# A hybrid trunk on one core: nine instead of eight of the eleven swiglu blocks by seven products, in another order and with other filling

## The chip, the core and the metric

The kernel runs on one core of a Trainium2 chip. The metric is the device time of one execution in microseconds, as the median of several runs. Clock and contention are read from the profile of one execution.

## What is computed

A trunk of two layers works on 256 frames of 2048 numbers, in float32. The first layer mixes tokens by gated linear attention, the second by an indexer with top-k attention; after each mixer comes a swiglu block. The change touches the swiglu alone:

```python
D_MODEL = 2048
SEQ = 256
D_FF = 5632

def swiglu(h, w1, w3, w2):
    return (jax.nn.silu(h @ w1) * (h @ w3)) @ w2

for i in range(2):
    h = rmsnorm(x, norm_mix[i])
    x = x + mixer(h)                  # i = 0: linear attention, i = 1: sparse attention
    x = x + swiglu(rmsnorm(x, norm_ffn[i]), ffn_w1[i], ffn_w3[i], ffn_w2[i])
return rmsnorm(x, norm_final)
```

## The kernel before

**Three matmuls for one.** Every float32 operand is split into a rounded part `h` and the rest `l`, and a product is computed as h·h + h·l + l·h. For a weight tile of 512 rows and 512 columns (1 MB, one tile `raw` of 128 partitions by 2048 numbers) `split_w` (L133) casts `wh` on ScalarE (L137) and subtracts `wl` on VectorE (L138). There are three buffers for each of `wh` and `wl`, and four for `raw`. Weights are loaded by SP's queue, each weight as often as it is used.

**The blocks of the swiglu.** The 5632 columns of w1 and w3 are eleven blocks of 512. For each block the kernel needs two products of the frames (two tiles of 128) with a 2048 by 512 weight. There are two ways to them:

- A *plain* block (`plain_steps`, L458): for w1 and then w3, four weight tiles each; each tile is multiplied with both frame tiles. That is 2 x 4 units of 24 matmuls (2 frame tiles, 4 rows of 128, 3 terms), 192 in all, with 8 weight splits. The results stand in the PSUM tiles `half`. In the eighth unit the block is gated on VectorE (L490 to L492), then turned by TensorE (L501) and split into the tile `g` by ScalarE (L507) and VectorE (L508).
- A *pair* block (`pair`, L373): w1 and w3 are computed at once, by a scheme that needs seven products instead of eight. Its products, in the order A11, F5, F3, A12, F6, N7, N22, are named after the form of the frames that is multiplied. Each is 2 weight tiles with 12 matmuls each (L398), so 168 in all, with 14 splits. Between products the weights are added up: the tiles `va` (w1, upper half) and `vb` (w3, upper half) get big sums on VectorE behind A11 (L411) and F3 (L415), two each, and accumulating transfers on GpSimd's queue into `va` behind F5 and F6 (L419), two each. The loads for the pair (`v`, `g3` and `raw`) are issued at L385. The two sets of homes, v0/v1 and v2/g3, change places from pair to pair, so the next pair's first weight can be loaded when N7 has split its tiles, and the second when N22 has.

**Down.** The product with w2 is done in pieces (`pieces`, L516): for each of four column groups, ScalarE copies x into the two PSUM tiles `down` (L521), each block of the piece adds 24 matmuls (L531 to L533, one weight split), and ScalarE copies the sums back to x (L538). A unit of a piece is one block on one column group, 24 matmuls and one split. The last block's part is done after the stage by `residual`.

**The order.** All of this is written out by hand in `ffn` (L541). `turns` lists the pair blocks; each entry names the block, the slots behind which a filling unit is run, and the items whose units join the waiting list: a number is a plain block, a tuple is a piece with these blocks. Slot 0 is behind A11, slot 6 behind N22, slot 7 is the end of the turn, -1 is ahead of A11. Units are taken from the list in order, so a turn may use units of an item of an earlier turn. A pair block is turned by TensorE (L220) in the turn that follows it, and split into `g0`, `g1` or `g2`, by the block's number modulo 3 (L222 on ScalarE, L223 on VectorE). A split is written in the program where its product or unit is; sums are queued behind the next split on VectorE (`sums_due`). On each engine instructions run in the order written by the scheduler.

Of the kernel before, what the change touches and what calls it, by code (L numbers as in the profile page):

```python
# [55 lines left out]
def trunk(  # L56
# [484 lines left out]
    def ffn(layer, nrm):  # L541
# [48 lines left out]
        def filler(item):  # L590

            if isinstance(item, int):
                return "plain", item, plain_steps((w1, w3), item, nrm.forms, sc, ready)
            return "piece", item, pieces(w2, [made[b] for b in item], ready)

        full = (0, 1, 2, 3, 4, 5, 6, 7)
        turns = ((0, (-1, -1, 0, 1, 2, 4, 5, 6), (1,)), (2, full, ((1, 0),)), (3, full, (4,)), (5, full, ((2, 3),)),
                 (6, full, ((4, 5),)), (7, full, (8,)), (9, full, ((6, 7),)), (10, full, ((8, 9),)))
        for turn, (b, at, items) in enumerate(turns):
            todo.extend(filler(i) for i in items)  # L600
            us = [None] * NT
# [501 lines left out]
    with tc.tile_pool(name="fz0", bufs=1) as fz:  # L1103
        n1.begin(fz)
        residual(gla_w_out[0], down, n1.update)
        down = ffn(0, n1)
        flush()
# [6 lines left out]
    with tc.tile_pool(name="fz1", bufs=1) as fz:  # L1114
        n3.begin(fz)
        residual(dsa_w_out[0], down, n3.update)
        down = ffn(1, n3)
        flush()
# [56 lines left out]
```

## Time and profile before

| | |
|---|---|
| median of 3 runs | 2228.13 us (2227.88 to 2228.15) |
| the profiled execution | 2227.94 us |
| its span, first to last instruction | 2226.2 us |
| mean granted TensorE clock | 0.999 |
| moved by DMA | 493.35 MB, mean 222 GB/s |
| weight splits on VectorE in the swiglus, raw, v and g (L138) | 193, 120 and 40 |
| pair matmuls (L398), plain (L475), pieces (L531 to L533) | 2688, 1152, 1920 |

The profile is of one execution. A group's row shows line, engine, operation, out<-in by the program's names, shape and count; behind the first bar the busy time in us and the mean length of one in ns; behind the second the idle time of the engine just ahead of them and what ended most of it. A row of the waits shows who waited for whom, the sum in us, how often and the longest. A row of the timeline shows start, length, engine, line and, in brackets, the idle time ahead. DMA issue rows show the size of one and the median time from issue to landing.

### The profile page before, as it was taken

What the parts mean: (1) busy time and instruction counts of PE and PEld (TensorE: products, weight loads), DVE (VectorE), ACT (ScalarE), POOL (GpSimd) and SP (SyncE); (2) the same over time, 40 slices, a digit from 0 to 9 for tenths busy, and PEclk for the clock granted to TensorE, in tenths of its full rate; (3) what the DMA queues carried; (4) which work ended last, traced back from release to release, by engine and by line L of the source; (5) the groups of instructions that cost most, each with busy time, mean ns of one, the idle gap of its engine ahead of it and who ended that gap; (6) DMA issues with size and microseconds to landing.
All of it is one profiled execution on the core that took longest, in us unless ns stands there. A gap on an engine that the chain in (4) does not pass through costs nothing.

```text
span 2226.2 us, 25148 instructions
## 1 busy us (share of the span) xinstructions
PE 2207.4 (99%) x10199; PEld 1828.2 (82%) x10199; DVE 1545.1 (69%) x1180; ACT 1289.2 (58%) x1248; POOL 111.3 (5%) x157
## 2 busy tenths in 40 slices
PE   9999999999999999999999999999999999999998
PEld 7888888888888888888888888888888888888886
DVE  6546546887777777877655755557877777787776
ACT  5545445666656665666544445456666666666664
POOL 0000000000000000000100000000000000000000
PEclk9999999999999999999999999999999999999999
DMA  8555465889879879777554554466997897897893
GB/s 293 172 170 178 135 229 179 263 224 314 222 228 307 221 229 315 211 228 231 194 183 142 178 173 159 164 204 196 298 243 238 276 247 228 281 261 214 281 245 114
DMA packets 254773, 493.35 MB, mean 222 GB/s; under 512 B 8201, under 2 KB 20833, under 8 KB 254529
## 3 DMA queue, kind: packets, MB, share of 16 engines
q1 hardware_dynamic: 219856, 423.33, 54.4%
q0 software_dynamic: 33792, 67.11, 17.3%
q8 instruction: 80, 1.31, 0.2%
q10 hardware_dynamic: 1008, 1.31, 0.2%
q14 instruction: 37, 0.30, 0.0%
HBM read 489.59 MB, written 2.12 MB: 221 GB/s over the span
## 4 chain that ended last, share of the span: by engine, by line
PE 95%; DVE 2%; ACT 1%; issue 1%; DMA 0%; SPq 0%; POOL 0%; POOLq 0%; ACTq 0%
PE acc L398 26%; PE half L475 11%; PE acc L206 11%; PE acc L208 11%; PE acc L207 11%; PE down L533 7%; PE down L532 6%; PE down L531 6%; PE tr L220 1%; DVE wl L138 1%; ACT wh L137 1%; PE trq L906 0%; PE po L765 0%; DVE v L411 0%; PE s L750 0%
## 5 line engine op out<-in xcount | busy, mean ns | idle before, releaser
L138 DVE TENSOR_TENSOR wl<-raw,wh 128x2048 fp32r<-128x2048 f32 x193 | 441.4, 2291 | 229.8 <-ACT wh L137 228.9
L197 DVE TENSOR_TENSOR wl<-raw,wh 128x2048 fp32r<-128x2048 f32 (+3 forms) x147 | 317.7, 2164 | 275.7 <-ACT wh L196 275.6
L137 ACT CAST wh<-raw 128x2048 fp32r<-128x2048 f32 x193 | 369.4, 1914 | 203.1 <-PE half L475 71.7
L196 ACT CAST wh<-raw 128x2048 fp32r<-128x2048 f32 (+3 forms) x147 | 265.1, 1807 | 221.1 <-PE acc L208 191.1
L206 PE MATMUL acc<-wh,hh 128*128 128x512 f32 (+3 forms) x832 | 325.4, 391 | 0.0
L208 PE MATMUL acc<-wh,hl 128*128 128x512 f32 (+3 forms) x832 | 317.3, 381 | 0.0
L207 PE MATMUL acc<-wl,hh 128*128 128x512 f32 (+3 forms) x832 | 316.4, 380 | 0.6 <-DVE wl L197 0.6
L138 DVE TENSOR_TENSOR wl<-v,wh 128x2048 fp32r<-128x2048 f32 x120 | 274.0, 2289 | 45.1 <-ACT wh L137 44.8
L137 ACT CAST wh<-v 128x2048 fp32r<-128x2048 f32 x120 | 229.7, 1914 | 71.6 <-PE acc L398 35.3
L532 PE MATMUL down<-wl,g 128*128 128x512 f32 x640 | 249.6, 390 | 1.1 <-DVE wl L138 1.1
L531 PE MATMUL down<-wh,g 128*128 128x512 f32 x640 | 249.6, 391 | 0.9 <-ACT g L507 0.9
L533 PE MATMUL down<-wh,g 128*128 128x512 f32 x640 | 248.5, 390 | 0.6 <-DVE g L508 0.6
L207 PEld LDWEIGHTS acc<-wl,hh 128*128 128x128 f32 x832 | 156.7, 188 | 29.6 <-issue 1.7
L208 PEld LDWEIGHTS acc<-wh,hl 128*128 128x128 f32 x832 | 156.3, 188 | 29.3
L206 PEld LDWEIGHTS acc<-wh,hh 128*128 128x128 f32 x832 | 156.5, 188 | 28.6 <-issue 1.9
L398 PE MATMUL acc<-wh,fhF 128*128 128x512 f32 x384 | 150.8, 393 | 0.0
L398 PE MATMUL acc<-wh,flF 128*128 128x512 f32 x384 | 149.9, 390 | 0.0
L398 PE MATMUL acc<-wl,fhF 128*128 128x512 f32 x384 | 149.6, 390 | 0.0
L532 PEld LDWEIGHTS down<-wl,g 128*128 128x128 f32 x640 | 120.2, 188 | 27.6 <-DVE wl L138 2.8
L531 PEld LDWEIGHTS down<-wh,g 128*128 128x128 f32 x640 | 120.2, 188 | 26.1 <-ACT g L507 1.5
L533 PEld LDWEIGHTS down<-wh,g 128*128 128x128 f32 x640 | 119.9, 188 | 26.2 <-DVE g L508 1.4
L206 PE MATMUL acc<-wh,g 128*128 128x512 f32 x312 | 123.3, 395 | 0.7 <-ACT g L222 0.7
(283 smaller groups left out, 3675.9 us busy)
## 6 DMA issues: line engine op xcount, KB each, us to landing
raw<-in_ffn_w SPq DMA_DIRECT2D x200, 1024.0 KB, 6.2
v<-in_ffn_w SPq DMA_DIRECT2D x48, 1024.0 KB, 8.4
v<-in_ffn_w POOLq DMA_DIRECT2D x48, 1024.0 KB, 9.9
raw<-in_dsa_w_in SPq DMA_DIRECT2D x48, 1024.0 KB, 4.9
raw<-in_gla_w_in SPq DMA_DIRECT2D x40, 1024.0 KB, 5.0
raw<-in_gla_w_out SPq DMA_DIRECT2D x16, 1024.0 KB, 5.0
g<-in_ffn_w SPq DMA_DIRECT2D x16, 1024.0 KB, 8.0
g<-in_ffn_w POOLq DMA_DIRECT2D x16, 1024.0 KB, 13.8
```

The costliest lines, as they stand in the source:

```text
L137: nc.scalar.copy(wh, raw)
L138: v = nc.vector.tensor_sub(wl, raw, wh.bitcast(F32))
L196: a = nc.scalar.copy(wh[:, sl, :n], raw[:, sl, :n])
L197: v = nc.vector.tensor_sub(wl[:, sl, :n], raw[:, sl, :n], wh[:, sl, :n].bitcast(F32))
L206: nc.tensor.matmul(acc[t][:, :n], hi[:, k, ts_], wh[:, k, :n], start=start, stop=False)
L207: nc.tensor.matmul(acc[t][:, :n], hi[:, k, ts_], wl[:, k, :n], start=False, stop=False)
L208: nc.tensor.matmul(acc[t][:, :n], lo[:, k, ts_], wh[:, k, :n], start=False, stop=last)
L398: nc.tensor.matmul(acc, l_[:, k, :], r_[:, j, :], start=start and k == i == 0, stop=stop and k == 7 and i == 2, skip_group_check=not start)
L475: nc.tensor.matmul(acc[bank], l_[:, k, :], r_[:, j, :], start=start and k == i == 0, stop=stop and k == 7 and i == 2, skip_group_check=not ...
L531: nc.tensor.matmul(acc[t], hi[:, k, ts_], wh[:, k, :], start=False, stop=False, skip_group_check=True)
L532: nc.tensor.matmul(acc[t], hi[:, k, ts_], wl[:, k, :], start=False, stop=False, skip_group_check=True)
L533: nc.tensor.matmul(acc[t], lo[:, k, ts_], wh[:, k, :], start=False, stop=last, skip_group_check=True)
```

## The change

`turns` is written anew. Nine blocks are pairs (0, 2, 3, 4, 6, 7, 8, 9, 10) and two are plain (1 and 5); before, eight were pairs and three plain (1, 4 and 8). The pieces are now (0), (1, 2), (3, 4), (5, 6), (7, 8) and (9); before they were (1, 0), (2, 3), (4, 5), (6, 7) and (8, 9). Most turns have six filling units, behind all products but A12; pair 0's turn and pair 2's have five behind products, none behind F5 and A12; pair 10's turn has eight. There are 56 units per layer where there were 64. The list is the same for both layers.

```diff
-        full = (0, 1, 2, 3, 4, 5, 6, 7)
-        turns = ((0, (-1, -1, 0, 1, 2, 4, 5, 6), (1,)), (2, full, ((1, 0),)), (3, full, (4,)), (5, full, ((2, 3),)),
-                 (6, full, ((4, 5),)), (7, full, (8,)), (9, full, ((6, 7),)), (10, full, ((8, 9),)))
+        five, six = (0, 2, 4, 5, 6), (0, 1, 2, 4, 5, 6)
+        turns = ((0, (-1, -1, 0, 2, 4, 5, 6), (1,)), (2, five, ((0,),)), (3, six, ((1, 2),)), (4, six, (5,)),
+                 (6, six, ((3, 4),)), (7, six, ()), (8, six, ((5, 6),)), (9, six, ((7, 8),)),
+                 (10, (0, 1, 2, 3, 4, 5, 6, 7), ((9,),)))
```

VectorE in pair 0's turn of the first layer, before, from F5's two splits on (`v2` and `g3` are va, `v0` and `v1` vb, `raw` with L138 in turn a unit's tile, F3's two, a unit's, A12's two):

```order
L138 TENSOR_TENSOR wl_3115<-v2_3030,wh_3114 128x2048
L138 TENSOR_TENSOR wl_3132<-g3_3032,wh_3131 128x2048
L138 TENSOR_TENSOR wl_3153<-raw_3150,wh_3152 128x2048
L138 TENSOR_TENSOR wl_3188<-raw_3183,wh_3187 128x2048
L138 TENSOR_TENSOR wl_3204<-raw_3185,wh_3203 128x2048
L415 SCALAR_TENSOR_TENSOR v0_3034<-v0_3034,raw_3183 128x2048
L486 TENSOR_TENSOR early_2936<-early_2936,half_2938 128x512
L138 TENSOR_TENSOR wl_3225<-raw_3222,wh_3224 128x2048
L415 SCALAR_TENSOR_TENSOR v1_3036<-v1_3036,raw_3185 128x2048
L138 TENSOR_TENSOR wl_3258<-raw_3253,wh_3257 128x2048
L138 TENSOR_TENSOR wl_3274<-raw_3255,wh_3273 128x2048
```

The same place of the changed kernel:

```order
L138 TENSOR_TENSOR wl_3115<-v2_3030,wh_3114 128x2048
L138 TENSOR_TENSOR wl_3132<-g3_3032,wh_3131 128x2048
L138 TENSOR_TENSOR wl_3155<-raw_3150,wh_3154 128x2048
L138 TENSOR_TENSOR wl_3171<-raw_3152,wh_3170 128x2048
L415 SCALAR_TENSOR_TENSOR v0_3034<-v0_3034,raw_3150 128x2048
L138 TENSOR_TENSOR wl_3190<-raw_3187,wh_3189 128x2048
L415 SCALAR_TENSOR_TENSOR v1_3036<-v1_3036,raw_3152 128x2048
L138 TENSOR_TENSOR wl_3226<-raw_3221,wh_3225 128x2048
L138 TENSOR_TENSOR wl_3242<-raw_3223,wh_3241 128x2048
L486 TENSOR_TENSOR early_2936<-early_2936,half_2938 128x512
```

The unit's split between F5 and F3 is gone, and the plain block's L486 has moved behind A12's splits.

ScalarE at the same place, before, from F3's first cast on (L485 and L487 are the plain block's silu, with the load of a table of functions; L434 copies F5's result):

```order
L137 CAST wh_3187<-raw_3183 128x2048
L434 COPY u_3148<-acc_3113 128x512
L137 CAST wh_3203<-raw_3185 128x2048
L485 ACT_TABLE_LOAD
L485 ACTIVATE early_2936<-half_2937,rstd_3109 128x512
L137 CAST wh_3224<-raw_3222 128x2048
L487 ACTIVATE early_2936<-early_2936,rstd_3109 128x512
L137 CAST wh_3257<-raw_3253 128x2048
L137 CAST wh_3273<-raw_3255 128x2048
L137 CAST wh_3291<-v2_3030 128x2048
L137 CAST wh_3308<-g3_3032 128x2048
```

And in the changed kernel:

```order
L137 CAST wh_3154<-raw_3150 128x2048
L137 CAST wh_3170<-raw_3152 128x2048
L434 COPY u_3148<-acc_3113 128x512
L137 CAST wh_3189<-raw_3187 128x2048
L137 CAST wh_3225<-raw_3221 128x2048
L137 CAST wh_3241<-raw_3223 128x2048
L485 ACT_TABLE_LOAD
L485 ACTIVATE early_2936<-half_2937,rstd_3109 128x512
L137 CAST wh_3259<-v2_3030 128x2048
L487 ACTIVATE early_2936<-early_2936,rstd_3109 128x512
L137 CAST wh_3276<-g3_3032 128x2048
```

The silu and its table have moved from behind F3's casts to between A12's casts and F6's (`v2_3030` and `g3_3032`).

ScalarE at the end of the first layer's swiglu, before (the last two units are two blocks on one column group; `wh` with L196 is the first weight tile of `residual`; L222 is the split of block 10, turned by TensorE behind the last unit):

```order
L538 COPY x02_85<-down0_7108 128x512
L521 COPY down0_7241<-x03_87 128x512
L538 COPY x12_86<-down1_7109 128x512
L137 CAST wh_7247<-raw_7245 128x2048
L521 COPY down1_7242<-x13_88 128x512
L137 CAST wh_7277<-raw_7275 128x2048
L561 ACTIVATE acc_6808<-acc_6808,rq_3111 128x512
L196 CAST wh_7338<-raw_7336 128x2048
```

And in the changed kernel, where these units are two column groups of the piece (9):

```order
L137 CAST wh_7311<-raw_7309 128x2048
L561 ACTIVATE acc_6830<-acc_6830,rq_3111 128x512
L196 CAST wh_7372<-raw_7370 128x2048
...
L538 COPY x02_85<-down0_7269 128x512
L521 COPY down0_7305<-x03_87 128x512
L538 COPY x12_86<-down1_7270 128x512
L222 CAST g1_7341<-tr_7342 128x512
L521 COPY down1_7306<-x13_88 128x512
```

The four copies between two column groups, which stood ahead of the last two units, now stand between them, with one of block 10's splits ahead of the last copy.

## Prediction

> **What bounds the kernel now.** First the page, for the share of each engine and the chain of waits:
>
> ```profile
> span 2226.2 us, 25148 instructions
> PE 2207.4 (99%) x10199; PEld 1828.2 (82%) x10199; DVE 1545.1 (69%) x1180; ACT 1289.2 (58%) x1248; POOL 111.3 (5%) x157
> ...
> PE 95%; DVE 2%; ACT 1%; issue 1%; DMA 0%; SPq 0%; POOL 0%; POOLq 0%; ACTq 0%
> ```
>
> TensorE is busy 99% of the span and is 95% of the chain, so a matmul that goes away should shorten the run by its own pitch, as long as its neighbours are not late. The pitch is read from TensorE's timeline in the block of pair 3, at the first of A11's 24 matmuls and the first of the unit behind them; the transposes of a turned block follow inside that unit:
>
> ```profile
> 561.78 0.39 PE L398 MATMUL acc<-wh,fhA 128*128 128x512 f32 x1
> ...
> 567.22 0.39 PE L475 MATMUL half<-wh,fhA 128*128 128x512 f32 x1
> ...
> 568.59 0.60 PE L220 MATMUL tr<-ident,u 128*128 128x128 f32 x4
> 568.94 0.48 PE L475 MATMUL half<-wh,fhA 128*128 128x512 f32 x1
> ```
>
> 24 matmuls take 567.22 - 561.78 = 5.44 us, 0.2267 us each; the 0.39 us of a row is its length in the pipeline, not its price. A product, and a filling unit, are 24 matmuls each.
>
> Second, TensorE's own waits, because they are what a new order can add or take away:
>
> ```profile
> PE down L532 <- DVE wl L138: 1.1, 4, 0.3
> PE down L531 <- ACT g L507: 0.9, 2, 0.4
> PE acc L206 <- ACT g L222: 0.7, 2, 0.3
> ...
> PE down L533 <- DVE g L508: 0.6, 2, 0.3
> ...
> PE tr L220 <- DVE g L508: 0.3, 1, 0.3
> ```
>
> These eleven belong to the two swiglu stages and their ends: 3.6 us of idle time. The idle time starts only when the 0.39 us of the matmul before is over, so each cost 0.39 - 0.23 = 0.16 us more: 3.6 + 11 x 0.16 = 5.4 us. Third, how much room is below TensorE, from the windows of pair 0's turn (six filling units, none behind A12) and of a later turn with eight:
>
> ```profile
> 406.10:476.80 70.70, 70.70 (x313) 58.55 (x312) 57.91 (x31) 44.30 (x29) 5.38 (x4) 1.00 0.93 279
> ...
> 728.60:811.10 82.50, 82.50 (x369) 68.35 (x368) 62.27 (x33) 53.83 (x46) 5.16 (x4) 1.00 0.85 255
> ```
>
> The columns after the length are busy us of PE, PEld, DVE, ACT and POOL, then clock, DMA share, GB/s. Pair 0's turn already has the spacing that the change gives to the others, and TensorE is busy through all of it at clock 1.00; but VectorE is at 82% and the DMA engines at 93%.
>
> **The change part by part.** *The matmuls.* A pair block has 7 x 24 = 168, a plain block 8 x 24 = 192; per swiglu one plain block becomes a pair, so 24 go per layer and 48 in all: 48 x 0.2267 = 10.9 us, all on the path. The 56 units that are left (of 64) are the same work. The Trainium skill, TensorE: Matmul & The Clock Gate, section Back-to-back issue gap, gives about 131 ns as the sustained spacing at N=512; by it 48 matmuls would be 6.3 us. The trace's 0.2267 us decides here, and the sum goes by it.
>
> *What VectorE and ScalarE get.* A pair has 14 weight splits and four big sums, a plain block 8 splits:
>
> ```profile
> L138 DVE TENSOR_TENSOR wl<-raw,wh 128x2048 fp32r<-128x2048 f32 x193 | 441.4, 2291 | 229.8 <-ACT wh L137 228.9
> L137 ACT CAST wh<-raw 128x2048 fp32r<-128x2048 f32 x193 | 369.4, 1914 | 203.1 <-PE half L475 71.7
> ...
> L521 ACT COPY down<-x 128x512 f32<-128x512 f32 x80 | 47.3, 591 | 15.5 <-DVE early L490 12.1 <-DVE early L491 2.4
> L538 ACT COPY x<-down 128x512 f32<-128x512 f32 x80 | 46.7, 584 | 108.0 <-PE down L533 107.1
> L411 DVE TENSOR_TENSOR v<-v,v 128x2048 f32<-128x2048 f32 x16 | 36.5, 2284 | 0.0
> ...
> L222 ACT CAST g<-tr 128x512 fp32r<-128x512 f32 x40 | 22.7, 586 | 15.3 <-PE tr L220 15.0
> ```
>
> Per layer that is 10 x 2.29 = 23 us more for VectorE and 6 x 1.91 = 11.5 us for ScalarE, and 16 copies of 0.59 us, since two pieces now have one part. With six units a turn VectorE has 20 splits and four sums, 24 x 2.29 = 55 us, beside 312 x 0.2267 = 70.7 us of matmuls: it fits, as in pair 0's turn. So these cost nothing on average, and the question is single places, where a split can't be ready two weight tiles ahead. There are three.
>
> *A: pair 0's turn, where the unit behind F5 goes.* VectorE and ScalarE there now:
>
> ```profile
> 425.07 2.29 DVE L138 TENSOR_TENSOR wl<-raw,wh 128x2048 fp32r<-128x2048 f32 x1 [0.91 <-ACT wh L137]
> 427.28 2.28 DVE L415 SCALAR_TENSOR_TENSOR v<-v,raw 128x2048 f32<-128x2048 f32 x1
> 429.49 0.68 DVE L486 TENSOR_TENSOR early<-early,half 128x512 f32<-128x512 f32 x1
> 430.08 2.28 DVE L138 TENSOR_TENSOR wl<-raw,wh 128x2048 fp32r<-128x2048 f32 x1
> ...
> 441.68 1.92 ACT L137 CAST wh<-g 128x2048 fp32r<-128x2048 f32 x1 [0.80 <-PE acc L398]
> ...
> 443.63 2.29 DVE L138 TENSOR_TENSOR wl<-g,wh 128x2048 fp32r<-128x2048 f32 x1 [0.43 <-ACT wh L137]
> ```
>
> With three buffers a cast starts when TensorE is done three weight tiles earlier, and its subtraction 443.63 - 441.68 = 1.95 us behind it. Today F3's second split follows a long unit and starts early. Let F3's matmuls start at 0: without the unit, its second half's cast waits for F5's first half to end, at -2.7; subtraction from -0.6 to 1.6 (VectorE's pitch is 427.28 - 425.07 = 2.2), sum to 3.8, the next unit's subtraction to 6.0. TensorE wants it with that unit's second matmul, at 5.44 + 0.23 = 5.7. That and the handover make 0.4 to 0.5 us late. Behind A12 the plain block's first silu now falls where A12 and F6 follow each other without a unit, and with it a table load; the cast of A12's second half also waited for its load:
>
> ```profile
> 425.41 1.28 ACT L485 ACT_TABLE_LOAD   x1 [0.36 <-PE half L475]
> 426.70 0.69 ACT L485 ACTIVATE early<-half,rstd 128x512 f32<-128x512 f32 x1
> ...
> 436.00 1.91 ACT L137 CAST wh<-raw 128x2048 fp32r<-128x2048 f32 x1 [0.64 <-DMA raw<-in_ffn_w]
> ...
> raw<-in_ffn_w SPq DMA_DIRECT2D x200, 1024.0 KB, 6.2
> ...
> g<-in_ffn_w POOLq DMA_DIRECT2D x16, 1024.0 KB, 13.8
> ```
>
> From that load on (itself 6.2 us, beside an accumulating transfer of up to 13.8), cast, table load, silu and F6's cast are 1.9 + 1.3 + 0.7 + 1.9 = 5.8 us in a row on ScalarE, and F6's subtraction comes 0 to 1.1 us late, as the load lands 5 us after its issue or behind the accumulation. I take 0.9, since the row shows the load already waited for. What F6's other half and the next unit's cast queue behind this adds up to 0.6 at most. A is 0.5 + 0.9 = 1.4 us, between 0 and 2.2.
>
> *B: pair 2's turn.* Two products without a unit between them meet two L223 and three early pieces (0.6 us pitch, row 429.49) on VectorE. Counted from A11's start, the first unit's subtraction ends at 1.95 + 2.2 + 0.1 = 4.3 us (its cast waits for the unit before A11); then VectorE has 7 big passes and 5 small ones up to the unit behind F3, 7 x 2.2 + 5 x 0.6 = 18.4 us, and is done at 22.7. TensorE wants it after A11, unit, F5 and F3 with four groups of four transposes (568.94 - 568.59 = 0.35 us each): 4 x 5.44 + 1.4 + 0.2 = 23.4. It is not late by itself, but ScalarE's two copies into the unit's sums stand ahead of a cast. I take 0.3 us, between 0 and 2.0 (the two waits of this turn now, with some more).
>
> *F: the stage's end.* Piece (9) has one part, so its units behind N22 are two column groups in a row, on the same two sums. Behind the last but one, L538 must empty each sum and L521 fill it before its matmuls: L538, L521, L538, L222, L521, 0.58 + 0.59 + 0.58 + 0.59 + 0.59 = 2.9 us from some 0.4 before that unit's end (its first sum is done three matmuls early). The second sum is ready 2.5 us after the end; TensorE, with six transposes (0.5) and three matmuls (0.7), would be at it after 1.2. I take 1.3 us, between 0.5 and 1.9. The block is turned earlier, so L206's wait at the end should go; it is in the 5.4 us.
>
> *Costed at nothing, at most 0.5 us a layer together.* From plain block to piece in pair 6's turn N7, which has no sums, covers the early passes. Block 6 takes the buffer g0 while piece (3, 4) still reads block 3 in it, so its two L222 wait on ScalarE behind N22's casts for that piece; behind them wait only the next unit's cast and what follows it, and that cast waits for the same unit anyway: 0.1 + 2 x 0.59 + 1.95 + 2.2 = 5.4 us after it, against 5.44 + 0.23.
>
> *The moved transfers.* Each load and each accumulation moves with its product, SP's queue and POOL's keep their order but for the plain block's eight loads a layer:
>
> ```profile
> v<-in_ffn_w SPq DMA_DIRECT2D x48, 1024.0 KB, 8.4
> v<-in_ffn_w POOLq DMA_DIRECT2D x48, 1024.0 KB, 9.9
> ```
>
> The next pair's second weight is loaded when N22 has split the old one, and added behind A11: N22, unit, A11 are 3 x 5.44 = 16 us for 8.4. F5's accumulations have four products and units until F6, 22 us, at worst for 13.8; from F6 to N22 nothing changes. SP waits for v in front of raw loads that are four buffers ahead. So none of it is on the path, unless transfers stretch: the last rival.
>
> *What goes.* The old places of the eleven waits (plain to piece at F5) are gone with the old order: -5.4 us, at least 0.
>
> Sum: 2227.94 (the profiled execution: span 2226.2 and 1.74 around it) - 10.9 - 5.4 + 2 x (1.4 + 0.3 + 1.3) = 2217.6; the median of the runs is 0.2 above that execution, so 2217.8. With all added terms at their tops, 2 x 6.6 = 13.2, it is 2224.8; with none, 2211.6.
>
> **The rivals.** *Nothing new is late* (the bottoms of A, B and F): 2211.6 plus 0.2, 2211.8. For it: pair 0's turn shows no wait now. Against: A is worked out from just that turn with one unit fewer.
>
> *Small lateness at every column group.* The unit behind a finished column group is split just in time:
>
> ```profile
> 526.79 2.29 DVE L138 TENSOR_TENSOR wl<-raw,wh 128x2048 fp32r<-128x2048 f32 x1 [3.51 <-ACT wh L137]
> ...
> 529.37 0.39 PE L532 MATMUL down<-wl,g 128*128 128x512 f32 x1
> ```
>
> It ends at 529.08, 0.29 us ahead. There are 24 such units per layer afterwards (20 before). If ScalarE's queue, with fewer units to catch up in, costs each 0.5 us, 0.2 of it shows: 48 x 0.2 = 9.6 us, 2227.4: no change. Against: the cast there waits for TensorE, not for the queue's backlog.
>
> *Slower: transfers take the lead.* Turn by turn a pair needs eight loads and four accumulating transfers in about 70.7 us instead of 82.5. Pair 0's window is 93% of its length, 65.8 us of transfer time; a later turn has one load fewer. If in a row of such turns that grew past 70.7 us, each would wait, at F6 and N22 for the accumulated halves and at A11 for the next pair's. At 1.5 us in each of 16 turns it gives 2217.8 + 24 = 2241.8; it decides from about 72 us of transfers a turn. For it: the window's 93%. Against: that window ran without a wait on TensorE. The Trainium skill, DMA: Bandwidth & Descriptors, section Bandwidth, puts the limit of one core's HBM at about 358 GB/s; 279 GB/s in that window is below it, so by the page there is room, while the engines' share of 93% says there is little.
>
> *The change does not do what it says*: the order could have kept the stages' length by moving matmuls. It has 48 fewer on TensorE, so I give it 0.01, at no change.
>
> **How the numbers follow.** A measurement of this kernel can tell about 0.2%, 4.5 us, from no change. My forecast has 0.66, nothing new late 0.12: both faster, 0.78. Small lateness 0.16 and the change without effect 0.01: the same, 0.17. Transfers: 0.05, slower. The range has to hold the forecast with its bounds, nearly to 2211.6 below and to 2224.8 above; from 2213 to 2225 it leaves out the transfers, the small lateness and part of the case with nothing late.
>
> **What would show it.** Right: in the groups 3024 matmuls of L398 for 2688 and 768 of L475 for 1152; each swiglu stage shorter by about 5 us; TensorE waits on a wl at the unit behind F3 in pair 0's turn, and on L521 at the stage's end; DMA share near 0.9 in the turns without a wait on v or g. Wrong: TensorE waits in most turns on wl, a chain with more than 2% of DVE or ACT, or wh casts that wait for v or g transfers.

## The result, and the profile after

| | before | after |
|---|---|---|
| median of the runs (4 each) | 2228.01 us (2227.86 to 2228.15) | 2215.59 us (2215.48 to 2216.34) |
| the profiled execution, its span | 2227.94, 2226.2 us | 2215.48, 2213.7 us |
| ratio of the runs, 95% interval | | 0.9945 (0.9933 to 0.9957) |

The change takes 12.4 us off: 2.2 us more than forecast, inside the range, and faster by more than 0.2%. The page of the changed kernel, first the span, the engines and the chain:

```profile
span 2213.7 us, 25142 instructions
PE 2195.1 (99%) x10151; PEld 1819.4 (82%) x10151; DVE 1589.8 (72%) x1200; ACT 1326.8 (60%) x1294; POOL 121.6 (5%) x165
...
PE 96%; DVE 1%; ACT 1%; issue 1%; DMA 1%; SPq 0%; POOL 0%; POOLq 0%; ACTq 0%
```

TensorE has 10151 matmuls and transposes for 10199, 48 fewer, and stays 99% busy. VectorE went from 69% to 72%. Next the windows of the two swiglu stages, from the first unit's matmul to the first L206 behind them. Columns as in the prediction: length, busy us of PE, PEld, DVE, ACT and POOL, clock, DMA share, GB/s. Before:

```profile
394.30:1062.14 667.84, 665.95 (x2977) 549.35 (x2975) 515.05 (x285) 424.29 (x344) 43.51 (x38) 1.00 0.84 251
1527.64:2195.27 667.63, 666.00 (x2978) 549.40 (x2976) 514.84 (x285) 424.26 (x344) 42.67 (x34) 1.00 0.84 250
```

And after; the third row is the turn of pair 4, the fourth 9 us of pair 0's turn, to which we come back:

```profile
394.15:1055.63 661.48, 660.01 (x2953) 545.23 (x2952) 538.02 (x295) 442.31 (x365) 48.68 (x42) 1.00 0.88 259
1521.13:2182.75 661.62, 660.04 (x2954) 545.27 (x2952) 538.01 (x295) 442.52 (x366) 47.84 (x38) 1.00 0.88 259
620.00:691.60 71.60, 71.60 (x324) 59.32 (x322) 59.08 (x33) 45.29 (x33) 5.16 (x4) 1.00 0.91 268
424.00:433.00 9.00, 9.00 (x41) 7.43 (x40) 8.82 (x5) 2.89 (x3) 0.00 (x0) 1.00 1.08 292
```

The stages are 6.4 and 6.0 us shorter: all of the gain is there. In a later turn TensorE is busy for 71.60 of 71.60 us, with the DMA engines at 91%. What TensorE waits for in the stages:

```profile
PE acc L398 <- DVE wl L138: 1.6, 2, 0.8
PE acc L398 <- ACT u L434: 1.4, 2, 0.7
```

The eleven waits of before are gone. Four new ones stand in their place, two in each layer, both in pair 0's turn. TensorE's timeline around them, F3's first matmul and F6's second:

```profile
422.06 0.39 PE L398 MATMUL acc<-wh,flF 128*128 128x512 f32 x1
423.13 0.50 PE L398 MATMUL acc<-wh,fhF 128*128 128x512 f32 x1 [0.68 <-ACT u L434]
423.46 0.39 PE L398 MATMUL acc<-wl,fhF 128*128 128x512 f32 x1
...
439.85 0.39 PE L398 MATMUL acc<-wh,fhF 128*128 128x512 f32 x1
441.01 0.50 PE L398 MATMUL acc<-wl,fhF 128*128 128x512 f32 x1 [0.77 <-DVE wl L138]
```

From start to start F3's matmul comes 1.07 us behind the one before, 0.84 more than the pitch; F6's 1.16, 0.93 more. In the second layer they are 0.84 and 0.95, and A12's second half is 0.26 late: 3.8 us in all. So the sum is -10.9 - 5.4 + 3.8 = -12.5 us, which is the difference of the spans. That it closes to the tenth is in part chance: terms of 0.1 to 0.2 us are left out of it, such as 0.1 us at the matmul behind each wait, of the old ones and of the new.

F3's wait is for a PSUM bank. F3 goes on in the bank b2 that holds F5's result, and L434 must first copy that result out. Before, a unit stood between F5 and F3 and gave it the time. F6's wait has ScalarE ahead of it; its timeline from F3's end on:

```profile
422.49 0.59 ACT L434 COPY u<-acc 128x512 f32<-128x512 f32 x1 [0.80 <-PE acc L398]
...
432.92 1.91 ACT L137 CAST wh<-raw 128x2048 fp32r<-128x2048 f32 x1 [4.81 <-DVE wl L138]
434.85 1.28 ACT L485 ACT_TABLE_LOAD   x1
436.15 0.69 ACT L485 ACTIVATE early<-half,rstd 128x512 f32<-128x512 f32 x1
436.74 1.89 ACT L137 CAST wh<-v 128x2048 fp32r<-128x2048 f32 x1
```

The cast of A12's second tile starts after 4.81 us of idle time. Two things end at 432.8 us, just ahead of it: VectorE's subtraction of A12's first tile, which the row names, and the load of the second tile; e9 will tell them apart. Behind the cast stand the table load, the plain block's silu and F6's first cast, without a gap, as the prediction had them. The first theory after the result was therefore: **the bank** (L434) makes F3 late, and **the table load** makes F6 late. The rival: not the table, but **A12's second weight tile** is late, and the table only adds to it. The Trainium skill, ScalarE: Activation LUTs, section What ACT_TABLE_LOAD costs, gives 1283 ns for the load, as here, and some 1380 ns of drain besides; no row here shows a drain, since the silu starts 0.02 us behind the load.

### The profile page after: what moved, and what is told of

The parts are those of the page before. It is cut to its first block, busy times and chain, and to the rows that moved or that the text cites. A ratio compares the mean times of both kernels' runs of the same rounds, so it can differ in the third digit from the quotient of the medians.

```text
span 2213.7 us, 25142 instructions
## 1 busy us (share of the span) xinstructions
PE 2195.1 (99%) x10151; PEld 1819.4 (82%) x10151; DVE 1589.8 (72%) x1200; ACT 1326.8 (60%) x1294; POOL 121.6 (5%) x165
## 4 chain that ended last, share of the span: by engine, by line
PE 96%; DVE 1%; ACT 1%; issue 1%; DMA 1%; SPq 0%; POOL 0%; POOLq 0%; ACTq 0%
PE acc L398 30%; PE acc L206 11%; PE acc L208 11%; PE acc L207 11%; PE half L475 7%; PE down L531 7%; PE down L532 7%; PE down L533 7%; PE tr L220 1%; PE trq L907 0%; PE po L766 0%; DVE wl L138 0%; PE s L751 0%; ACT wh L137 0%; PE po L1080 0%
## 5 line engine op out<-in xcount | busy, mean ns | idle before, releaser
L138 DVE TENSOR_TENSOR wl<-raw,wh 128x2048 fp32r<-128x2048 f32 x185 | 422.7, 2291 | 196.4 <-ACT wh L137 196.1
L137 ACT CAST wh<-raw 128x2048 fp32r<-128x2048 f32 x185 | 353.9, 1913 | 172.8 <-PE half L475 54.2
L196 ACT CAST wh<-raw 128x2048 fp32r<-128x2048 f32 (+3 forms) x147 | 265.3, 1807 | 214.4 <-PE acc L208 190.2
L138 DVE TENSOR_TENSOR wl<-v,wh 128x2048 fp32r<-128x2048 f32 x132 | 301.3, 2288 | 36.5 <-ACT wh L137 35.4
L206 PE MATMUL acc<-wh,hh 128*128 128x512 f32 (+3 forms) x832 | 325.4, 391 | 0.0
L137 ACT CAST wh<-v 128x2048 fp32r<-128x2048 f32 x132 | 252.5, 1915 | 72.5 <-PE acc L398 27.8
L531 PE MATMUL down<-wh,g 128*128 128x512 f32 x640 | 250.2, 391 | 0.0
L206 PEld LDWEIGHTS acc<-wh,hh 128*128 128x128 f32 x832 | 156.5, 188 | 28.5 <-issue 1.9
L398 PE MATMUL acc<-wh,fhF 128*128 128x512 f32 x432 | 169.9, 393 | 1.4 <-ACT u L434 1.4
L398 PE MATMUL acc<-wl,fhF 128*128 128x512 f32 x432 | 168.5, 390 | 1.6 <-DVE wl L138 1.6
L398 PE MATMUL acc<-wh,flF 128*128 128x512 f32 x432 | 168.3, 390 | 0.0
L531 PEld LDWEIGHTS down<-wh,g 128*128 128x128 f32 x640 | 120.1, 188 | 24.9 <-ACT down L521 0.4
L419 POOL DMA_DIRECT2D v<-in_ffn_w x52 | 67.3, 1294 | 1118.0 <-DVE wl L138 1118.0
## 6 DMA issues: line engine op xcount, KB each, us to landing
g<-in_ffn_w SPq DMA_DIRECT2D x18, 1024.0 KB, 10.9
```

The source lines that it names most:

```text
L137: nc.scalar.copy(wh, raw)
L138: v = nc.vector.tensor_sub(wl, raw, wh.bitcast(F32))
L196: a = nc.scalar.copy(wh[:, sl, :n], raw[:, sl, :n])
L206: nc.tensor.matmul(acc[t][:, :n], hi[:, k, ts_], wh[:, k, :n], start=start, stop=False)
L398: nc.tensor.matmul(acc, l_[:, k, :], r_[:, j, :], start=start and k == i == 0, stop=stop and k == 7 and i == 2, skip_group_check=not start)
L531: nc.tensor.matmul(acc[t], hi[:, k, ts_], wh[:, k, :], start=False, stop=False, skip_group_check=True)
```

## Experiments

Each kernel is the changed one with the edit shown (its main lines), except where it says otherwise; their line numbers can be a few higher. The medians of the kernel before were 2228.05, 2228.01, 2227.99 and 2228.03 us beside the four groups of runs, so the times can be set beside 2215.59.

| | median (lowest to highest), us | new TensorE waits in the stages |
|---|---|---|
| changed kernel | 2215.59 (2215.48 to 2216.34) | L434, F6 |
| e1 table early | 2213.82 (2213.35 to 2215.03) | L434, A12 in one layer |
| e2 F3 in its own bank | 2214.11 (2213.77 to 2214.82) | A12, 1.0 and 1.8 us |
| e3 e1 and e2 | 2214.81 (2213.02 to 2215.62) | A12, 0.7 us twice (fastest run) |
| e4 before, unit from F5 to A12 | 2232.42 (2232.14 to 2233.92) | L434, the unit behind A12 |
| e5 F3's sum early | 2216.31 (2215.95 to 2217.61) | L434, A12, F6, smaller ones |
| e6 e5 and e2 | 2216.04 (2215.59 to 2216.62) | A12, F6 |
| e7 one unit ahead of A11 | 2221.58 (2220.19 to 2223.12) | A11, the unit behind it, F6 |
| e8 ten pairs | 2317.81 (2315.41 to 2322.94) | 4.1 to 4.9 us at N22 in twelve turns, L434, smaller ones |
| e9 A12's second tile in g2 | 2212.72 (2212.54 to 2213.35) | L434, and one of 0.2 us |
| e10 e9 and e2 | 2211.04 (2210.82 to 2211.09) | none |
| e11 e9 and e6 | 2210.59 (2210.42 to 2211.73) | none |
| e12 e8, L450 earlier | 2264.03 (2262.08 to 2268.29) | many, none above 1.9 us |

**e1: the table loaded early.**

```diff
         todo = deque()
         made = {}
+        nc.scalar.activation(warm, x[1][2][:, 0:8], AF.Silu)
```

> The changed kernel with one small silu of 8 columns more per layer, in the mixer's tail, so that the table of functions is loaded about 60 us ahead of the plain block's first silu. Theory (the table load between A12's second cast and F6's first cast makes F6's split late): without the 1.28 us load F6's first subtraction ends about 0.9 us earlier, at the time when TensorE wants it, so both waits at F6 go and nothing else moves: 2 x 0.9 = 1.8 us less than the changed kernel, about 2213.8 us. Rival (the load of A12's second weight tile is what is late, and the table load only fills that time): F6's wait stays, 2215.6 us. Either way the wait of F3 for L434's copy stays at 0.68 us in each layer.

Measured 2213.82 us, on the theory's number: F6's waits are gone, L434's stay. But now one wait of 0.3 us is at A12's second half. So the table is one link of the chain, and its head is still open.

**e2: F3 in a bank of its own, in pair 0's turn.**

```diff
-        product(b2, vc, "F3", False, True, minus(vb, vc))
+        f3 = bank() if own else b2
+        product(f3, vc, "F3", own, True, minus(vb, vc))
...
-        nc.vector.tensor_add(w, w, b2)
+        nc.vector.tensor_add(w, w, f3)
+        if own:
+            nc.vector.tensor_add(w, w, y)
```

> The changed kernel, but in pair 0's turn F3's product has a PSUM bank of its own, and VectorE adds one term more to w. Theory (F3's first matmul waits for L434 to copy F5's result out of the same bank, and that wait pays for the late splits behind it): the two waits of 0.68 us for L434 are gone, but of their 0.84 us each only a part shows, since then the splits are late: 0.3 to 0.5 us at the unit behind F3, the lateness that the prediction had there, and at A12's second half, whose load lands at the same time as before whatever TensorE does. The silu stands ahead of A12's second cast in this kernel, so the wait at F6 moves there. In all 0.4 to 0.7 us less per layer, 2214.2 to 2214.8 us. Rival (the copy is a wait like any other and nothing is queued behind it): the full 2 x 0.84 = 1.7 us less, 2213.9 us, with F6's waits as they were and no new wait on a wl.

Measured 2214.11 us, 0.1 below the expected range. No wait for L434 is left, so the bank was its cause; but two waits of 1.0 and 1.8 us have come up at A12's second half, where the silu now stands ahead of the cast. Of what the bank gives, 2 x 0.84 us and 0.1 for each matmul behind, a part is eaten behind it, as the theory said.

**e3: both.** 

> Both edits together: F3 in its own PSUM bank in pair 0's turn, and the table of functions loaded in the mixer's tail. Theory (after both, only splits and A12's second load are in the way): no wait for L434, none at F6 but perhaps 0.1 us, and about 0.4 us late at the unit behind F3 or at A12's second half: 1.1 to 1.3 us less per layer than the changed kernel, 2213.0 to 2213.4 us, the fastest of the four. Rival (the two waits are independent and both go fully): 2 x (0.84 + 0.93) = 3.5 us less, 2212.1 us. If it is no faster than the table load alone, then what sets this turn is A12's second load.

Measured 2214.81 us as the median, but from 2213.02 to 2215.62: a wider spread than any kernel with so little waiting has here, and we didn't find its reason. The profiled execution is the one of 2213.02 us and has two waits of 0.7 us, both at A12's second half. With the table and the bank out of the way A12 is still late, which points to A12's second load, as the expectation's last sentence has it; with this spread the medians alone don't settle it. Independent waits that go fully are not what the trace shows.

**e4: the kernel before with the unit moved.**

```diff
-        turns = ((0, (-1, -1, 0, 1, 2, 4, 5, 6), (1,)), (2, full, ((1, 0),)), (3, full, (4,)), (5, full, ((2, 3),)),
+        turns = ((0, (-1, -1, 0, 2, 3, 4, 5, 6), (1,)), (2, full, ((1, 0),)), (3, full, (4,)), (5, full, ((2, 3),)),
```

> The kernel before, with one edit: in pair 0's turn the unit that stood behind F5 stands behind A12. So F5 and F3 follow each other as in the changed kernel, but A12 and F6 do not. Theory (without a unit between them F3 waits for L434's copy out of F5's bank): TensorE waits 0.68 us for L434 once in each layer, 0.84 us by the start of the matmul, none at F6 and none on a wl behind F3: 1.7 us slower than before, 2229.7 us. Rival (the prediction's: F3's second split and the unit's behind it are late): a wait on a wl of 0.3 to 0.5 us behind F3, none for L434, 0.9 us slower, 2228.9 us.

Measured 2232.42 us, slower than both said. TensorE's waits in pair 0's turn of the first layer:

```profile
PE half L475 <- DVE wl L138: 0.8, 1, 0.8
PE acc L398 <- ACT u L434: 0.7, 1, 0.7
```

L434's wait is there as the theory had it, and none at the unit behind F3. But there is also one of 0.8 us at the unit that now stands between A12 and F6. So F6 is not late because a unit is missing ahead of it, as the prediction argued: whatever comes behind A12 is late. What went missing is the unit ahead of F3, which also gave A12's loads 5.44 us. The four waits of both layers come to 3.1 us from start to start; the rest of the 4.4 us is not explained.

**e5 and e6: A12's second load issued earlier**, e6 with the bank as well. The load goes into the raw buffer that F3's first tile leaves, when F3's first sum has read it:

```diff
-        product(b2, vc, "F3", False, True, minus(vb, vc))
+        product(b2, vc, "F3", False, True, minus(vb, vc, first))
```

`minus` then writes the first of the two sums at once, not behind the next split.

> The changed kernel with one edit: in pair 0's turn the first of F3's two big sums on VectorE (L415, which reads F3's first weight tile) stands ahead of F3's first subtraction, where VectorE was idle for 1.7 us, and not behind its second one. The tile is then free 4.5 us earlier, and the load of A12's second weight tile into it is issued at about 421.8 us of the span, not at 426.3. Theory (A12's second load is what makes this place late, and the table load between A12's casts and F6's only adds to it): that load lands before its cast could start, the waits at A12's second half and at F6 are gone though the table is loaded where it was, and with the 0.2 to 0.4 us at A12 and 1.05 us at F6 that is 1.3 us per layer, 2.7 in all: 2212.9 us. Rival (the table load alone makes F6 late): F6's waits stay at 0.77 us, 2215.6 us. The wait of F3 for L434 stays in both.

> The same edit, and F3 in a PSUM bank of its own in pair 0's turn. Theory: no TensorE wait is left in the two swiglu stages, neither for L434 nor for a wl, since with the sum out of the way the unit's subtraction behind F3 is no longer late either: 0.95 us per layer less than with the sum alone, 2211.0 us, the fastest of all and near the case of the prediction in which nothing new is late (2211.8). Rival (the lateness moves on to another place, as it did when only the bank was changed): a wait on a wl of 0.5 to 1 us at the unit behind F3 or at A12, 2212 to 2213 us.

Both were no faster than the changed kernel, 2216.31 and 2216.04 us: the theory of the buffer fell. The load's issue (start, length, engine, line) and its time to landing, first in the changed kernel, with the second of F5's two accumulating transfers, the one into g, behind it:

```profile
426.27 0.37 SPq L385 DMA_DIRECT2D raw<-in_ffn_w  x1
...
raw<-in_ffn_w SPq DMA_DIRECT2D x1, 1024.0 KB, 6.5
...
g<-in_ffn_w POOLq DMA_DIRECT2D x1, 1024.0 KB, 12.6
```

Then with the sum early:

```profile
421.99 0.37 SPq L385 DMA_DIRECT2D raw<-in_ffn_w  x1
...
raw<-in_ffn_w SPq DMA_DIRECT2D x1, 1024.0 KB, 11.5
...
g<-in_ffn_w POOLq DMA_DIRECT2D x1, 1024.0 KB, 14.7
...
424.00:433.00 9.00, 9.00 (x41) 7.42 (x40) 6.92 (x4) 3.02 (x2) 0.00 (x0) 1.00 1.09 284
```

Issued 4.3 us earlier, it landed at 421.99 + 11.5 = 433.5 us of the span, for 426.27 + 6.5 = 432.8. The DMA engines are full from 424 to 433 us in both kernels (shares of 1.08 and 1.09), mostly with F5's accumulating transfers; a plain load issued into that takes its share away from the one into g (14.7 us for 12.6) and is itself no sooner. So the theory for the next kernels: it is **the order of the transfers**. A12's second load must be issued ahead of the accumulations, not only ahead of its place.

**e7: one unit ahead of A11 only, and the unit back behind F5.**

```diff
-        turns = ((0, (-1, -1, 0, 2, 4, 5, 6), (1,)), ...
+        turns = ((0, (-1, 0, 1, 2, 4, 5, 6), (1,)), ...
```

> The changed kernel with pair 0's unit back behind F5, and only one unit ahead of A11. Theory (a unit between F5 and F3 covers L434's copy and the late splits, and what was won ahead of A11 is lost there): no wait for L434, and none or little at F6, 2 us less per layer; but A11's second weight tile, whose load is issued late in the mixer's tail, is late by about 1.9 us per layer, a wait of TensorE on the wl of a g tile at A11: 2215.6 us, no change. Rival (that load would be there in time): 2211.5 us.

Measured 2221.58 us, slower by 6.0. The wait at A11 is there (1.2 us), but behind it, within the unit, one of 2.1 us for a cast, and F6's wait of 0.7 us is still there. That the stage's start has no room is shown; but its price was put at about half (1.9 us a layer, where TensorE lost 1.4 us from start to start at A11 and 2.2 behind it), and that a unit behind F5 would clear F6 was wrong.

**e8: ten pairs**, with four units in most turns.

```diff
+        four = (0, 2, 4, 6)
+        turns = ((0, (-1, -1, 0, 2, 4, 5, 6), (1,)), (2, (0, 2, 4, 5, 6), ((0,),)), (3, four, ((1, 2),)), (4, four, ()),
+                 (5, four, ((3, 4),)), (6, four, ()), (7, four, ((5, 6),)), (8, four, ()),
+                 (9, (0, 2, 4, 5, 6), ((7, 8),)), (10, (0, 1, 2, 4, 5, 6, 7), ((9,),)))
```

> Ten blocks by seven products, only block 1 plain, with four filling units in most turns (behind A11, F3, F6 and N22), five or seven in the others: 48 matmuls fewer again, 10.9 us, and about 62 us of matmuls per turn. Theory (below TensorE there is no room for this): the transfers of a turn, some 60 us of the DMA engines' time by the changed kernel's windows, and the splits no longer fit; the halves that are accumulated behind F6 come 14 us after their issue and are split about 1.6 us late at N22, so TensorE waits on a wl at N22 and A11 in seven turns per layer, 22 us or more in all: slower than the changed kernel by 5 to 20 us, 2220 to 2235 us. Rival (only single places count, as the prediction had it, and transfers are hidden): 2215.6 - 10.9 + some 5 us for waits like those of pair 0's turn, 2205 to 2210 us.

Measured 2317.81 us, slower by 102: the direction was expected, the size by far not. TensorE's waits, and a window over five of its turns:

```profile
PE down L531 <- ACT wh L137: 52.0, 12, 4.9
PE acc L398 <- ACT u L434: 10.8, 16, 0.7
PE acc L398 <- DVE wl L138: 8.1, 18, 0.8
...
620.00:980.00 360.00, 331.43 (x1409) 265.65 (x1408) 276.88 (x147) 216.44 (x171) 28.37 (x22) 0.97 0.84 239
```

One wait repeats in twelve turns, for 52 of the 72 us. The DMA engines are at 84%, less than in the changed kernel: on the average there is room. The place is N22; TensorE's and VectorE's rows there in one turn, and the accumulating transfer of the half of `va` that N22 needs last:

```profile
731.76 0.60 PE L220 MATMUL tr<-ident,u 128*128 128x128 f32 x4
736.84 0.73 PE L531 MATMUL down<-wh,g 128*128 128x512 f32 x2 [4.48 <-ACT wh L137]
737.96 0.79 PE L398 MATMUL acc<-wh,fhN 128*128 128x512 f32 x1 [0.39 <-DVE u L450]
...
735.02 2.29 DVE L138 TENSOR_TENSOR wl<-g,wh 128x2048 fp32r<-128x2048 f32 x1 [4.27 <-ACT wh L137]
737.23 0.68 DVE L450 TENSOR_TENSOR u<-u,acc 128x512 f32<-128x512 f32 x1
...
g<-in_ffn_w POOLq DMA_DIRECT2D x1, 1024.0 KB, 14.9
```

N22's first matmul waits for L450, which takes N7's result out of the bank that N22 goes on with. L450 stands on VectorE behind the subtraction of N22's second half, and that half lands 14.9 us after its transfer was issued behind F6. Between F6 and N22 now stand N7 and one unit, where the changed kernel has N7 and two, and that is too short. Two matmuls of the next unit (L531) were put ahead of N22 and wait too, for a cast that stands behind that half's cast on ScalarE; most of the idle time is counted there. So two ways lead from the late half to TensorE, and they end about 1 us apart.

The wait has an aftermath. TensorE's granted clock (the column behind POOL's) in the 4.2 us behind it:

```profile
736.80:741.00 4.20, 3.77 (x9) 2.73 (x10) 3.31 (x3) 0.00 (x0) 0.00 (x0) 0.59 1.05 406
```

From 741 to 745 us it is 1.00 again. Behind the waits that end at 666, 806 and 874 us it is 0.50, 0.61 and 0.50 in the same 4.2 us.

**e9, e10, e11: A12's second tile in g2.** This buffer is free until block 2 is turned, so its load can be issued before F5's accumulating transfers. e10 adds the own bank, e11 the early sum too.

```diff
-        vd = load(wa, 1, stream)
+        vd = load(wa, 1, (stream[0], (res, "g2", 1) if first else stream[1]))
```

> The changed kernel with one edit: in pair 0's turn A12's second weight tile is loaded into g2, which is free until block 2 is turned, and not into the raw buffer that F3's first tile leaves. Its load then needn't wait for that buffer and is issued ahead of F5's two accumulating transfers, where the DMA engines stand idle around 410 us of the span. Theory (formed from the kernel whose sum was early: there the load was issued 4.3 us earlier and landed no earlier, since the DMA engines were busy with the accumulating transfers until 432 us; so it is the order of the transfers that makes A12's second load, and behind it the silu with its table and F6's split, late): the tile is there by 420 us, the waits at A12's second half (0.2 to 0.4 us) and at F6 (1.05 us) go though the table stays where it is, 1.3 us per layer, 2212.9 us. Rival 1 (the table load alone makes F6 late): F6's waits stay, 2215.6 us. Rival 2 (transfer time is only handed on): the accumulations end some 2.5 us later, and TensorE waits for a wl of the accumulated g tile at F6, 2215 to 2217 us. The wait for L434 stays in all.

> The same home for A12's second tile, and a PSUM bank of its own for F3 in pair 0's turn. Theory: with that load early, what the bank alone could not give is given: no wait for L434, none at A12 and F6; the unit behind F3 is split up to 0.45 us late, which other matmuls moved ahead of it cover, as they did in the kernel with the bank and the early table: 2.2 us per layer less than the changed kernel, 2211.2 us. Rival (the lateness moves on again): a wait on a wl of 0.5 us or more at the unit behind F3 or at F6, 2212 to 2214 us.

> All three edits of pair 0's turn: A12's second tile in g2, F3 in its own PSUM bank, and F3's first sum ahead of F3's subtractions. Theory: no lateness is left even behind F3, 2211.0 us, the fastest with the one before, and within 1 us of it. Rival (the early sum costs something by itself, as in the two kernels with it that were no faster): 1 us or more slower than the kernel before this one, with a wait on a wl at F3 or at the unit behind it.

Measured 2212.72, 2211.04 and 2210.59 us, each within 0.5 us of the theory's number. ScalarE in e9 at the same place, from the cast of A12's second tile on:

```profile
428.99 1.92 ACT L137 CAST wh<-g 128x2048 fp32r<-128x2048 f32 x1 [0.80 <-PE acc L398]
431.76 1.28 ACT L485 ACT_TABLE_LOAD   x1 [0.84 <-PE half L475]
433.05 0.69 ACT L485 ACTIVATE early<-half,rstd 128x512 f32<-128x512 f32 x1
434.43 1.92 ACT L137 CAST wh<-v 128x2048 fp32r<-128x2048 f32 x1 [0.69 <-PE half L475]
```

The cast now waits for TensorE alone and starts 3.9 us earlier. It also starts ahead of VectorE's subtraction of A12's first tile (430.62 us here), so that was not what held it before: the load was. Table and silu stand where they stood in the order, and F6's cast waits for TensorE too. That the table alone makes F6 late is refuted: it takes both, the late load and the table behind it, and F6's wait goes when either is moved (e1, e9). Refuted is rival 2 as well: the accumulating transfers were issued 0.7 us later and landed at most 0.8 us later. e10 is 1.7 us faster than e9, twice the 0.84 us of L434's wait: with the load early, the bank gives its full price. e10 and e11 have no wait above 0.1 us in either stage and are the fastest: e11 against the kernel before 0.9923 (0.9911 to 0.9936), 5.0 us below the changed kernel. Between e10 and e11 the runs tell no difference.

**e12: ten pairs, with L450 ahead of that subtraction.**

```diff
-            for c in range(2):
-                wh, wl = split_w(raws[c])
+            for c in range(2):
+                with behind((first.ins,) if first is not None and c else ()):
+                    wh, wl = split_w(raws[c])
...
+        add = nc.vector.tensor_add(y, y, b3)
+        product(b3, va, "N22", False, True, None, add)
```

> The kernel with ten pairs, with one edit: in every pair L450, which takes N7's result out of the PSUM bank that N22 goes on with, stands ahead of the subtraction of N22's second half on VectorE, where it stood behind it. Theory (of the 102 us that ten pairs cost, most came from this: N22's first matmul waits for L450, L450 stands behind a subtraction, and that waits for the accumulating transfer of the g tile, which lands 14.9 us after its issue): N22 starts when N7 and the transposes are done, and waits only in its middle, for a wl, about 2.0 us; of some 5.2 us lost at N22 in each of twelve turns 3.1 go, 37 us in all, and the clock recovers a little: 2270 to 2282 us, still far slower than the changed kernel. Rival (the late half holds N22 in any case): no more than 10 us less, 2308 us or more.

Measured 2264.03 us: 54 us less, where 37 were expected, and below the expected range. The rival is wrong. In TensorE's order the unit's two matmuls no longer stand ahead of N22, so the edit took away both ways at once and doesn't tell them apart. What is left at N22 is the late half itself, 0.9 to 1.8 us a turn, and 0.4 us for L450. TensorE's waits, and the window of one of its turns:

```profile
PE acc L399 <- DVE wl L138: 25.8, 34, 1.8
PE acc L399 <- ACT u L435: 10.8, 16, 0.7
...
700.00:770.00 70.00, 66.85 (x294) 53.83 (x293) 55.42 (x29) 42.86 (x34) 5.16 (x4) 1.00 0.89 265
```

The clock is 1.00 where e8 had 0.97, over the whole run 0.998 for 0.987. The waits in the stages fell from 72 to 43 us, 29 us, less than expected; the clock's 1.1% of 2314 us is some 25 us, an estimate from the two means; together they are the 54. So the theory undervalued the clock; the clock was not changed by itself. The Trainium skill, TensorE: Matmul & The Clock Gate, section Why this matters for your kernels, warns of a slower clock from idle gaps of more than about 3 us. The two kernels agree with it: in the stages gaps of 4.1 to 4.9 us in e8, with the clock near half behind them, and none above 1.9 in e12.

## Why the prediction was right, point by point

- **The matmuls, -10.9 us: right.** 48 went, at the same pitch, and the whole difference closes with them. By the 131 ns of the Trainium skill, TensorE: Matmul & The Clock Gate, section Back-to-back issue gap, which the prediction set against the trace, 4.6 us of the gain would have no source.
- **The eleven old waits, -5.4 us: right**, all gone.
- **A, pair 0's turn, forecast 1.4 us a layer: measured 1.8 and 2.1**, below the top of 2.2. The step that failed is its first half, the 0.5 us of a late split at the unit behind F3. The lateness was computed rightly, but it isn't on the path. It can be seen where the bank is out of the way, in e10: TensorE's rows at the start of that unit

```profile
427.55 0.39 PE L478 MATMUL half<-wh,fhA 128*128 128x512 f32 x1
427.78 0.39 PE L478 MATMUL half<-wh,fhN 128*128 128x512 f32 x1
428.01 0.39 PE L398 MATMUL acc<-wh,fhA 128*128 128x512 f32 x1
428.29 0.50 PE L478 MATMUL half<-wl,fhA 128*128 128x512 f32 x1
```

  The unit's first matmul with wl stands 0.74 us behind its first, not 0.23: two matmuls that need no wl, one of A12's among them, were put in between, and the wait that is left is 0.05 us. In the changed kernel the wait for L434 covers the lateness as well. The step that the prediction lacked is that wait: F3 and F5 share a PSUM bank, and between them L434 needs about 1 us, which a unit used to give it. That cost 0.84 us a layer; e2 shows the cause. So it is luck that the first half came out near: a wait that the prediction didn't have stands in for one that isn't there.
- **A's second half, 0.9 us at F6: 0.93 and 0.95 measured**, at the place and through the chain that was named, load, cast, table, silu, cast. Its reason was half right. "Since the row shows the load already waited for" was the point: e9 removes the waits with the load alone and leaves the table. "Where A12 and F6 follow each other without a unit" was not: e4 has a unit there and waits all the same.
- **B, pair 2's turn, 0.3 us: nothing.** No wait is there. "It is not late by itself" was right, and the 0.3 us added to it were not needed.
- **F, the stage's end, 1.3 us: about 0.2**, below its own lower bound of 0.5. This is the term that was mis-sized most, 2.2 us over two layers. The copies run as worked out; ScalarE behind the last but one unit, and TensorE, from the transposes on:

```profile
1048.65 0.59 ACT L538 COPY x<-down 128x512 f32<-128x512 f32 x1 [2.27 <-PE down L533]
1049.27 0.59 ACT L521 COPY down<-x 128x512 f32<-128x512 f32 x1
...
1050.75 0.60 ACT L521 COPY down<-x 128x512 f32<-128x512 f32 x1
...
1049.13 0.82 PE L220 MATMUL tr<-ident,u 128*128 128x128 f32 x6
1049.91 0.50 PE L531 MATMUL down<-wh,g 128*128 128x512 f32 x1
...
1051.41 0.61 PE L531 MATMUL down<-wh,g 128*128 128x512 f32 x2
```

  From the first copy to the end of the last they take 2.7 us, to 1051.35. But TensorE doesn't come to the second sum after six transposes and three matmuls: seven matmuls of the first sum are put ahead, and it comes at 1051.6, just behind the copy. What is left is at the first sum: its first matmul stands at 1049.91, just behind the copy that fills it (to 1049.86), some 0.2 us later than six transposes would let it. The prediction took the order in which the program is written for the order on the engine.
- **What was costed at nothing** cost nothing: no other wait in the stages.
- **The rivals.** *Nothing new late* (2211.8) isn't what happened, but e10 and e11 show that it can be had, at 2211.0 and 2210.6. (By the bottoms that it names, F's 0.5 us would belong in it, 2212.8; its number leaves F out.) *Small lateness at every column group*: no wait on a `down` tile is left. *Transfers take the lead*: not turn by turn; the third window row shows TensorE without a gap at a DMA share of 0.91. Yet its mechanism decides at one place, A12's second load, for 9 us in which the engines are full. e8 shows that its turning point was put in the wrong measure: not 72 us of transfers a turn, but whether one accumulating transfer lands in the time between the products on both sides of it. The prediction cited a limit of about 358 GB/s from the Trainium skill, DMA: Bandwidth & Descriptors, section Bandwidth, by which there was room. This row of the changed kernel, from 433 us on, moves 402 GB/s, so that limit doesn't hold here. The same section gives about 358 GB/s as the share when both cores of an HBM domain stream, and its table, taken with one core alone, reaches 425 GB/s for large transfers; this kernel runs on one core, and the table is nearer:

```profile
433.00:441.00 8.00, 7.24 (x31) 5.37 (x29) 5.18 (x3) 7.97 (x7) 0.00 (x0) 1.00 1.05 402
```

So the forecast was 2.2 us too high: F and B were put 2.8 us too high in the two layers and A 1.0 too low, which makes 1.8; the other 0.4 us are not resolved. That the errors had opposite signs is luck.

## What to carry to other kernels

When work that stood between two products is moved, ask not only whether their operands are ready, but also who must still read the PSUM bank that the second goes on with, and whose transfers get less time. Count transfers place by place: here a load that shared the engines with accumulating transfers landed only behind them, though it was issued 4.3 us earlier; a buffer that let it go ahead of them helped. And read lateness from the order on the engine, where independent matmuls may have been put into the gap, not from the order in the program.

## What the runs showed of the hardware

- A wait of TensorE costs more than its idle time: 0.68 us idle at F3 made 0.84 us from start to start, and the next matmul then came 0.33 us behind, not 0.23 (423.13 to 423.46).
- From issue to landing an accumulating transfer of 1 MB took 9 us as the first of two and 12.6 to 14.9 as the second, issued some 2 us later, where plain loads ahead of them took 5.1 (e9, median of four); a plain load of 1 MB issued into them took 11.5 (e5). With accumulating transfers alone under way the DMA engines were full at 209 GB/s (424 to 428 us of the changed kernel), with plain loads alone at 402 (433 to 441).
- Waits of 4.1 to 4.9 us once a turn went with a granted clock of 0.987 over the run (e8), waits below 1.9 us with 0.998 (e12). In e8 the clock is 0.50 to 0.61 in the 4.2 us behind such a wait, and back at 1.00 in the next 4 us behind two of the four looked at, at 0.72 and 0.75 behind the others.
